# Values of a neighbourhood attention stored per head pair, and attention chunks of every m-th key

## The chip, the cores and the metric

The kernel runs on one core of a Trainium2 chip. The core has a matrix engine (TensorE: the profile has PE for its matmuls and PEld for its weight loads), VectorE (DVE), ScalarE (ACT), GpSimd (POOL), and SyncE (SP), which here issues nearly all transfers; 16 DMA engines carry them out. The metric is the device time of one execution in microseconds (us), the median of the runs.

## The reference, cut to what matters

One encoder layer is applied to a prompt of 256 positions and to a sample of 2048. The mixed positions stand in a grid of rows of 64 columns. Half of the width is a neighbourhood attention with 8 heads of 64 values: each query sees a window of 8 rows and 16 columns, cut out of slabs of keys.

```python
proj = h @ w_in                                   # q, k, v, z_a, u_f, z_f
logits = einsum('bjqhd,bijkhd->bhjqik', q_blk, k_slab) * scale
logits = where(valid, logits + bias, NEG_INF)
p = softmax(logits over all keys of the slab)
out = einsum('bhjqik,bijkhd->bjqhd', p, v_slab)   # y_a
y_f = fourier_mix(u_f, w_fourier, b_fourier)
mixed = concat([rms_norm(y_a, g_na) * silu(z_a), rms_norm(y_f, g_f) * silu(z_f)])
y = x + rms_norm(mixed @ w_out, g_post)
```

All of it is float32. The change lies in how `v` gets from the projection to the last einsum of the attention, and in how `p` is turned for it.

## The kernel before

The kernel has three parts in time. Up to about 600 us it computes the projections and the Fourier half. From 604 to 850 us it computes the attention, and beside it the output product of the Fourier half. The rest is the output product of the attention half, with norm and residual.

*v on its way.* The rows of v of the sample come out of the projection as tiles of 128 positions x 512 values. `put_rows` (L359) stores each of them in the DRAM tensor `vN`, whose layout is [column half, row, column, 512 values]: 16 stores of 128 runs of 2 KB. Six copies from DRAM to DRAM (`v_copy`, L366) then make one tensor `vD` for each of the four column blocks: 23, 31, 31 and 24 columns of the 32 rows, with all 512 values for a key. v of the prompt lies in `vP`, by other stores (L355).

*Passes and groups.* The attention runs in four passes, one for each pair of heads (`pr`, 128 of the 512 values). A pass has nine groups (`group`, L1162): the prompt, and then four row groups R = 0 to 3 with two column halves `hc` each. A group has 256 queries in two blocks `b`; a block sees `NR[R]` rows (11, 15, 15, 12) of a column block's 23, 31, 31 or 24 columns, that is 253 to 465 keys (160 for the prompt). 36 groups in all.

*A group's steps.* `prep` loads its queries four groups ahead. `prep_v` (L1183) loads v and the gate z_a. `scores` (L1211) multiplies queries and keys in PE into `s`; `bias_max` (DVE, L1247), `exps` (ACT, L1252) and `soft` (POOL, L1259) make of it the weights `w`, 128 queries in the partitions and the keys along the free dimension. `transp` (L1571) turns `w` in PE, one chunk of keys at a time, so that the keys stand in the partitions; ACT (L1579) and DVE (L1581) copy the result out of PSUM as `pt`. `pv` (L1586) multiplies it with v, whose keys stand in the partitions too, and DVE (L1607) takes the product to `y`.

*Chunks.* A block of n keys has m = 2, 3 or 4 chunks. Before, chunk x holds the keys z·x to z·x + z − 1, with z = n / m rounded up to a multiple of 8 and at most 128. The load takes the keys of one chunk into the partitions, and the chunks one behind the other in the free dimension: each packet is the 512 B of one key and one head pair, out of the key's 2 KB. Where the rows of `vD` don't reach to m·z keys, the last chunk is a load of its own (L1195; 12 of these, of 84 or 116 keys).

*Order.* PE, DVE, ACT, POOL and SP run in the order of the code, which the loop over k (L1816) writes out by hand. In step k stand the scores of group k, the transposes of group k−1 before and between matmuls of the Fourier half's output (`f_mm`, L1514, or `pairs`), and, late in the step, `pv` of group k−1 (L1907), then `prep_v` of group k+1 (L1917), `prep` of group k+4, and the stores that wait in `puts`. So a group's v is loaded about two steps before `pv` needs it; three buffers hold it (`VB`). All loads and stores of SP are one queue in order: `za`, `ql`, the tables `tb`, the parts `yr` and `yz` for the Fourier half and the stores `oD` and `yD` stand between the loads of v.

Of the kernel before, what the change touches and what calls it, by code (L numbers as in the profile page):

```python
# [10 lines left out]
F32 = mybir.dt.float32  # L11
# [19 lines left out]
K0 = (0, 4, 12, 20)  # L31
KW = (23, 31, 31, 24)
# [142 lines left out]
def build(tc, A, O):  # L175
    nc = tc.nc
# [3 lines left out]
    dr = es.enter_context(tc.tile_pool(name="dr", bufs=1, space=DRAM))  # L180
# [1 line left out]
    qD = dr.tile([4, 128, T], F32, name="qD")  # L182
    kD = dr.tile([4, 128, T], F32, name="kD")

    vD = [dr.tile([32, w, 512], F32, name="vD%d" % i) for i, w in enumerate(KW)]
    vP = dr.tile([2, 4, 40, 512], F32, name="vP")
    zD = dr.tile([2, 512, T], F32, name="zD")
    ZD = dr.tile([128, 16, 512], F32, name="ZD")
    uD = dr.tile([TP, 512], F32, name="uD")

    vN, uN = [dr.tile([2, 32, 32, 512], F32, name=n) for n in ("vN", "uN")]
    sD = dr.tile([5, 128, 4, 512], F32, name="sD")
    xD = dr.tile([7, 128, 4, 512], F32, name="xD")
    ivD = dr.tile([18, 128], F32, name="ivD")
# [5 lines left out]
    ident = cst.tile([128, 128], F32, name="ident")  # L200
# [24 lines left out]
    def mmt(n):  # L225
        x = mmc[0] % 5 > 2
        mmc[0] += 1
        return ps.tile([128, n], F32, tag="t" if x else "a", name="mm", bufs=2 if x else 3)
# [115 lines left out]
    def vu_out(m, c):  # L344
        s, b = PL[c]
        o = st.tile([128, 512], F32, tag="f", name=m + "o", bufs=3)
        x = row_tile(c)
        nc.scalar.activation(o, acc.pop((m, c)), AF.Copy, scale=invt[:, x:x + 1])
        if s is not None:
            put_rows(m, 0, b, s, o)  # L350
        elif m == "u":
            nc.sync.dma_start(uD[c * 128:c * 128 + 128, :], o)
        else:
            for r in range(4):
                nc.sync.dma_start(vP[c, r, 8 * c:8 * c + 32], o[32 * r:32 * r + 32])  # L355
                x = 24 * (1 - c)
                nc.sync.dma_start(vP[1 - c, r, 32 * c:32 * c + 8], o[32 * r + x:32 * r + x + 8])

    def put_rows(m, sg, b, s, o):  # L359
        r = 16 * sg + 4 * s  # L360
        nc.sync.dma_start((vN if m == "v" else uN)[b, r:r + 4].rearrange("r c e -> (r c) e"), o)


    VC = ((0, 0, 0, 23, 0), (1, 0, 8, 24, 0), (1, 1, 0, 7, 24), (2, 0, 24, 8, 0), (2, 1, 0, 23, 8), (3, 1, 8, 24, 0))

    def v_copy(i):  # L366
        x, b, c0, n, d0 = VC[i]
        nc.sync.dma_start(vD[x][:, d0:d0 + n], vN[b][:, c0:c0 + n])


    uu_ = {}
# [125 lines left out]
    def vu(sg, S, hooks):  # L497
# [7 lines left out]
        for i, (j, s) in enumerate(seq):  # L505
            for x in loads.get(i, ()):
                op_load(x)
            if i in splits:
                op_split(splits[i])
            for f in hooks.get(i, ()):  # L510
                f()
            p = mmt(512)
            h, l = op_[j]
            th, tl = bnew[sg, j]
            for k in range(4):
                mm3(nc, p, th[:, k, 128 * s:128 * s + 128], tl[:, k, 128 * s:128 * s + 128], h[k // 2][:, k % 2],
                    l[k // 2][:, k % 2], k == 0, k == 3)
            T2 = lambda o, a: nc.vector.tensor_tensor(out=o, in0=a, in1=p, op=ALU.add)
            if j == 0:
                uc[s] = et("uc")  # L520
                nc.scalar.copy(uc[s], p)
            elif j == 2:
                T2(uc[s], uc[s])
            elif j == 3:
                u4[s] = et("u4")
                T2(u4[s], uc[s])
            else:
                o = st.tile([128, 512], F32, tag="f", name="vuo", bufs=3)
                T2(o, (u4 if j in (4, 6) else uc)[s])
                if j == 4:  # L530
                    T2(uc[s], uc[s])
                put_rows("v" if j in (1, 6) else "u", sg, int(j in (4, 6)), s, o)
# [104 lines left out]
    for kp in range(4):  # L637
        ks = slice(2 * kp, 2 * kp + 2)
        v = part(RV[kp // 2], kp)
# [131 lines left out]
    for b in range(16):  # L771
# [13 lines left out]
        if 2 <= b < 8:  # L785
            x, y = divmod(b, 2)
# [9 lines left out]
        p = mmt(512)[:, :TP]  # L796
# [3 lines left out]
        o = st.tile([128, 256], F32, tag="f", name="f", bufs=3)  # L800
        if kind % 2:
            i, d = p, o
        else:
            i = p.rearrange("p (b r c) -> p b r c", b=2, c=32)
            d = o.rearrange("p (r b c) -> p b r c", b=2, c=32)
# [47 lines left out]
    for i in range(16):  # L853
        sg, pr = divmod(i, 8)
# [14 lines left out]
        o = [st.tile([128, 1024], F32, tag="f", name="f", bufs=3) for x in range(2)]  # L869
# [31 lines left out]
        for j in range(7):  # L901
            for f, d in ((u_load, 0), (u_split, 4), (u_stage1, 6)):
                x = 7 * pr + j - 7 - d
# [33 lines left out]
            if sg == 0:  # L937
                x, y = divmod(7 * (pr - 1) + j, 14)
# [27 lines left out]
            if 9 <= i < 15 and j == 2:  # L966
                v_copy(i - 9)
            p = mmt(512)
# [34 lines left out]
    ptb = [ps.tile([128, 512], F32, tag="t", name="ptb", bufs=2) for i in range(2)]  # L1003
# [179 lines left out]
    def prep_v(g):  # L1183
        cs = slice(g["pr"] * 128, g["pr"] * 128 + 128)
        g["v"] = jl.tile([128, 7, 128], F32, tag="v", name="v", bufs=VB)
        g["ch"], j = [], 0
        for b, (c0, w) in enumerate(g["t"]):
            n = g["nr"] * w
            src = (vP[b] if g["R"] is None else vD[2 * g["hc"] + b][K0[g["R"]]:]).rearrange("r c e -> (r c) e")
            m = -(-n // 128)  # L1190
            z = min(-(-n // m) + 7 & ~7, 128)
            f = m if src.shape[0] >= m * z else n // z
            nc.sync.dma_start(g["v"][:z, j:j + f], src[:z * f, cs].rearrange("(j p) e -> p j e", p=z))
            if f < m:
                nc.sync.dma_start(g["v"][:n - z * f, j + f], src[z * f:n, cs])  # L1195
            ch = [(z * x, min(z, n - z * x), j + x) for x in range(m)]
            g["ch"].append(ch)
            j += len(ch)
        g["za"] = jl.tile([128, 256], F32, tag="za", name="za", bufs=VB)
        nc.sync.dma_start(g["za"], zD[1, cs, g["ts"]])  # L1200

# [69 lines left out]
    for g in G[:2]:  # L1271
        prep(g)
        prep_v(g)
# [11 lines left out]
    for t, (g, x) in enumerate(zip(G, (0, 640))):  # L1285
        g["w"] = []
        for c0, w in g["t"]:
            n = 2 * g["nr"] * w
# [281 lines left out]

    def transp(g, b):  # L1571
        ch = g["ch"][b]
        n, z = len(ch) * 128, ch[0][1]
        o = jp.tile([128, 2, 512], F32, tag="pt", name="pt", bufs=PB)
        for h in range(2):
            for j, (c0, nk, v) in enumerate(ch):
                nc.tensor.transpose(ptb[h][:nk, j * 128:j * 128 + 128], g["w"][b][:, h, c0:c0 + nk], ident)  # L1577
            if h == 0:
                nc.scalar.copy(o[:z, h, :n], ptb[h][:z, :n])  # L1579
            else:  # L1580
                V.tensor_copy(o[:z, h, :n], ptb[h][:z, :n])  # L1581
        g["pt"] = g.get("pt", []) + [o]
# [109 lines left out]
    def part(P, name, n):  # L1692
        return [sm.tile([128, n, 128], F32R, tag="y%s%d" % (x, n) if n < 4 else "y" + x, name="y" + x,
                        bufs=3 if n == 4 else 1) for x in "hl"]
# [103 lines left out]
    prep(G[4])  # L1798
    f_mm(0)
    transp(G[0], 0)  # L1800
    f_norm(range(2))
    transp(G[0], 1)
    soft(G[1], 1)
    run_later()
# [4 lines left out]
    pv(G[0])  # L1809
    ys_load(ftiles[2])  # L1810
    prep_v(G[2])
    split_q(G[3])
    prep(G[5])
    ones32 = sm.tile([128, 32], F32, name="ones32", bufs=1)
    nc.vector.memset(ones32, 1.0)
    for k in range(2, len(G) + 1):  # L1816
        pr, i = divmod(k, 9)
        g, f = G[k] if k < len(G) else None, G[k - 1] if k else None
# [14 lines left out]
        if k == 28:  # L1833
            for c, x in enumerate(("kh", "kl")):
                w = kp.tile([128, T], F32R, tag=x, name="wk")
                WO[c] = [w[:, 56 + D * y:56 + D * y + D] for y in range(2)]
        if k in WK:
            c, y = WK[k]
# [3 lines left out]
        x = k // 2 + 1  # L1842
# [11 lines left out]
        if not g:  # L1854
            a_mm(atiles[0], 0, range(6))
        transp(f, 0)
        if g:
            exps(g, 0, 1)
# [57 lines left out]
        if k + 1 < len(G):  # L1916
            prep_v(G[k + 1])  # L1917
# [123 lines left out]
```

## Time and profile before

| | |
|---|---|
| Median of 3 runs | 959.88 us (959.08 to 960.82) |
| The profiled execution | 958.19 us |
| Its span, first to last instruction | 956.4 us |
| Granted PE clock, mean | 0.997 |
| PE busy (matmuls) | 944.8 us, 99% |
| DVE, ACT, POOL busy | 732.0, 505.8, 453.3 us |
| DMA | 272.17 MB in 140790 packets, mean 285 GB/s |
| Transposes of `w` (L1577) | 440 |

The profile is one execution. Its lines name an engine, an operation, the tiles (out<-in) and the shapes. Weight loads overlap matmuls, so the bars of both add up to more than the time. A line with "x48 | 8.2, 171 | 0.0" stands for 48 instructions, 8.2 us busy, 171 ns each, 0.0 us of idle time before them. "DMA share" is the mean busy share of the 16 DMA engines.

### The profile page before, as it was taken

How to read it: one execution, taken by the hardware profiler on the slowest of the kernel's cores; microseconds unless marked ns; L12 is line 12 of the kernel's file. 1: busy time of each engine (PE TensorE's matmuls, PEld its weight loads, DVE VectorE, ACT ScalarE, POOL GpSimd, SP SyncE). 2: the span in 40 equal slices, each digit the busy share in tenths (PEclk: the TensorE clock that was granted, in tenths of full speed). 3: DMA queues.
4: the chain of work that ended last, by engine and by line, in shares of the span. 5: the costliest groups of instructions: out<-in, count | busy, mean ns of one | idle time of the engine just before them, and what ended most of it. 6: DMA issues, size and time to landing. Idle time of an engine off the chain costs nothing.

```text
span 956.4 us, 16730 instructions
## 1 busy us (share of the span) xinstructions
PE 944.8 (99%) x5595; PEld 784.3 (82%) x5595; DVE 732.0 (77%) x1347; ACT 505.8 (53%) x1088; POOL 453.3 (47%) x426
## 2 busy tenths in 40 slices
PE   9999999999999999999999999999999999999996
PEld 7889988888888888888888879788787888788885
DVE  6758987788876765698887369777888878759876
ACT  6835676433334532233344267677876777654443
POOL 4100002464751302575566045567899798624444
PEclk9999999999999999999999999999999999999998
DMA  9899697557848894499889996698998999889995
GB/s 356 298 385 336 243 339 270 189 201 270 299 188 323 314 341 144 175 352 361 300 289 338 338 341 246 215 276 281 309 253 253 290 280 312 239 296 327 305 317 197
DMA packets 140790, 272.17 MB, mean 285 GB/s; under 512 B 12854, under 2 KB 80664, under 8 KB 137440
## 3 DMA queue, kind: packets, MB, share of 16 engines
q1 hardware_dynamic: 140352, 270.68, 82.9%
q8 instruction: 45, 0.74, 0.3%
q10 hardware_dynamic: 288, 0.40, 0.1%
q14 instruction: 41, 0.34, 0.1%
q0 software_dynamic: 64, 0.02, 0.0%
HBM read 181.37 MB, written 96.81 MB: 291 GB/s over the span
## 4 chain that ended last, share of the span: by engine, by line
PE 89%; DMA 4%; DVE 2%; POOL 2%; ACT 1%; issue 1%; SPq 0%; DVEq 0%; POOLq 0%; ACTq 0%
PE mm L166 18%; PE mm L164 18%; PE mm L165 18%; PE po L1504 10%; PE ptb L1577 5%; PE pv L1593 5%; PE s L1225 4%; DMA yr<-yD 2%; PE px L1689 2%; PE pz L1689 2%; DMA yo<-xt 1%; PE py L164 1%; PE py L165 1%; PE py L166 1%; PE ptb L1043 1%
## 5 line engine op out<-in xcount | busy, mean ns | idle before, releaser
L164 PE MATMUL mm<-xh,wa 128*128 128x512 f32 x448 | 174.4, 389 | 0.0
L166 PE MATMUL mm<-xh,wa 128*128 128x512 f32 x448 | 174.3, 389 | 0.0
L165 PE MATMUL mm<-xl,wa 128*128 128x512 f32 x448 | 174.3, 389 | 0.0
L545 POOL TENSOR_TENSOR ws<-wr 128x512 f32<-128x512 f32 x16 | 22.6, 1415 | 219.3 <-DMA wr<-wz 215.6
L1259 POOL TENSOR_SCALAR w<-w,m 128x465 f32<-128x465 f32 (+9 forms) x136 | 89.3, 670 | 32.7 <-DVE m L1256 13.5
L165 PEld LDWEIGHTS mm<-xl,wa 128*128 128x128 f32 x448 | 84.1, 188 | 17.5
L164 PEld LDWEIGHTS mm<-xh,wa 128*128 128x128 f32 x448 | 84.1, 188 | 17.5
L166 PEld LDWEIGHTS mm<-xh,wa 128*128 128x128 f32 x448 | 84.1, 188 | 17.4
L560 DVE TENSOR_TENSOR wa<-wr,wa 128x512 fp32r<-128x512 f32 x60 | 75.4, 1264 | 21.9 <-ACT wa L559 21.6
L1504 PE MATMUL po<-wk,yh 128*128 128x512 f32 x280 | 87.1, 392 | 0.9 <-ACT yh L1490 0.9
L1252 ACT ACTIVATE w<-w,m 128x465 f32<-128x465 f32 (+9 forms) x136 | 78.4, 579 | 14.3 <-DVE m L1247 13.6
L1968 POOL TENSOR_TENSOR xt<-of,xt 128x512 f32<-128x512 f32 x34 | 43.2, 1293 | 54.6 <-issue 33.0
L1247 DVE CUSTOM_DVE_ANT_1 w<-s,tb 128x465 f32<-128x465 f32 (+8 forms) x124 | 61.4, 529 | 8.9 <-PE s L1225 8.0
L598 POOL TENSOR_TENSOR mt<-mt,rmask 128x880 f32<-128x880 f32 (+2 forms) x24 | 50.3, 2111 | 32.6 <-DVE mt L594 26.2
L164 PE MATMUL mm<-vh,xh 128*128 128x512 f32 x168 | 65.4, 389 | 0.0
L165 PE MATMUL mm<-vl,xh 128*128 128x512 f32 x168 | 65.4, 389 | 0.0
L166 PE MATMUL mm<-vh,xl 128*128 128x512 f32 x168 | 65.4, 389 | 0.0
L1504 PEld LDWEIGHTS po<-wk,yh 128*128 128x128 f32 x280 | 52.1, 188 | 12.2 <-ACT yh L1490 1.3
L891 DVE TENSOR_TENSOR f<-u,mm 128x512 f32<-128x512 f32 x64 | 43.4, 679 | 23.3 <-PE mm L166 18.5
L1577 PE MATMUL ptb<-ident,w 128*120 128x128 f32 (+8 forms) x422 | 59.0, 277 | 1.4 <-ACT pt L1579 1.2
L559 ACT CAST wa<-wr 128x512 fp32r<-128x512 f32 x60 | 36.5, 618 | 43.5 <-PE mm L166 20.4
L1577 PEld LDWEIGHTS ptb<-ident,w 128*120 128x120 f32 (+8 forms) x422 | 47.1, 140 | 14.5 <-issue 4.6
(332 smaller groups left out, 2469.3 us busy)
## 6 DMA issues: line engine op xcount, KB each, us to landing
wr<-wz SPq DMA_DIRECT2D x48, 512.0 KB
vl<-sD SPq DMA_DIRECT2D x20, 512.0 KB
xm<-xm SPq DMA_DIRECT2D x9, 1024.0 KB
oD<-ofs SPq DMA_DIRECT2D x18, 512.0 KB
of<-oD SPq DMA_DIRECT2D x18, 512.0 KB
xt<-xn SPq DMA_DIRECT2D x18, 512.0 KB
yo<-xt SPq DMA_DIRECT2D x35, 256.0 KB
yr<-yD SPq DMA_DIRECT2D x34, 256.0 KB
```

The source lines that it names most:

```text
L164: nc.tensor.matmul(out, lh, rh, start=first, stop=False)
L165: nc.tensor.matmul(out, lh, rl, start=False, stop=False)
L166: nc.tensor.matmul(out, ll, rh, start=False, stop=last)
L560: nc.vector.tensor_tensor(out=o[:, 1], in0=src, in1=o[:, 0].bitcast(F32), op=ALU.subtract)
L598: nc.gpsimd.tensor_tensor(out=o, in0=i, in1=rmask[:, m0:m0 + n].unsqueeze(2).to_broadcast([128, n, 80]), op=ALU.add)
L891: nc.vector.tensor_tensor(out=dst(f, b), in0=src(uu[u]), in1=src(p), op=op)
L1247: nc.vector.tensor_tensor_reduce(out=rows(g["w"][b][:, h, :n], w), in0=rows(g["s"][2 * b + h][:, :nr * sw(w)], sw(w))[:, :, :w], in1=tv, s ...
L1252: nc.scalar.activation(w, w, AF.Exp, bias=m[:, h:h + 1], scale=-1.0, accum_out=m[:, 2 + h:3 + h])
L1259: nc.gpsimd.tensor_scalar(w, w, m[:, 4 + h:5 + h], 1.0, ALU.mult, ALU.mult)
L1504: nc.tensor.matmul(p, (d["l"] if x == 2 else d["h"])[:, c], w(n, int(x == 1), c), start=j == 0, stop=j == 11)
L1577: nc.tensor.transpose(ptb[h][:nk, j * 128:j * 128 + 128], g["w"][b][:, h, c0:c0 + nk], ident)
L1593: nc.tensor.matmul(p[hs, b], g["v"][:nk, v, hs], g["pt"][b][:nk, h, j * 128:j * 128 + 128], start=j == 0, stop=j == len(ch) - 1)
```

## The change

`vN` and `vD` get the head pair as an outer dimension: [column half, 4, row, column, 128] and [4, row, column, 128]. A key's values for one pair are 512 B as before, but the next key's follow directly. `put_rows` stores a tile of v in four runs of 512 B per position. The tensor for u keeps its layout.

Chunk x of a block now holds every m-th key, beginning with key x. Partition p of the load has the keys p·m to p·m + m − 1, which lie side by side in `vD`: a packet has 2 to 4 keys, 1 to 2 KB. The prompt's `vP` isn't changed, and its packets stay at 512 B. The number of partitions is n / m rounded up to an even number, in place of a multiple of 8. There is one load for each block.

The transposes read every m-th column of `w`, and an even number of them, where the tile's width leaves room for the one more (in the first two groups it doesn't always).

```diff
-    vD = [dr.tile([32, w, 512], F32, name="vD%d" % i) for i, w in enumerate(KW)]
+    vD = [dr.tile([4, 32, w, 128], F32, name="vD%d" % i) for i, w in enumerate(KW)]
...
-    vN, uN = [dr.tile([2, 32, 32, 512], F32, name=n) for n in ("vN", "uN")]
+    vN = dr.tile([2, 4, 32, 32, 128], F32, name="vN")
+    uN = dr.tile([2, 32, 32, 512], F32, name="uN")
...
     def put_rows(m, sg, b, s, o):
         r = 16 * sg + 4 * s
-        nc.sync.dma_start((vN if m == "v" else uN)[b, r:r + 4].rearrange("r c e -> (r c) e"), o)
+        if m == "v":
+            nc.sync.dma_start(vN[b, :, r:r + 4].rearrange("h r c e -> (r c) h e"), o.rearrange("p (h e) -> p h e", h=4))
+        else:
+            nc.sync.dma_start(uN[b, r:r + 4].rearrange("r c e -> (r c) e"), o)
...
         x, b, c0, n, d0 = VC[i]
-        nc.sync.dma_start(vD[x][:, d0:d0 + n], vN[b][:, c0:c0 + n])
+        nc.sync.dma_start(vD[x][:, :, d0:d0 + n], vN[b][:, :, c0:c0 + n])
...
             n = g["nr"] * w
-            src = (vP[b] if g["R"] is None else vD[2 * g["hc"] + b][K0[g["R"]]:]).rearrange("r c e -> (r c) e")
             m = -(-n // 128)
-            z = min(-(-n // m) + 7 & ~7, 128)
-            f = m if src.shape[0] >= m * z else n // z
-            nc.sync.dma_start(g["v"][:z, j:j + f], src[:z * f, cs].rearrange("(j p) e -> p j e", p=z))
-            if f < m:
-                nc.sync.dma_start(g["v"][:n - z * f, j + f], src[z * f:n, cs])
-            ch = [(z * x, min(z, n - z * x), j + x) for x in range(m)]
-            g["ch"].append(ch)
-            j += len(ch)
+            z = -(-n // m) + 1 & ~1
+            if g["R"] is None:
+                src = vP[b].rearrange("r c e -> (r c) e")
+                nc.sync.dma_start(g["v"][:z, j:j + m], src[:, cs].rearrange("(p j) e -> p j e", j=m))
+            else:
+                src = vD[2 * g["hc"] + b][g["pr"]].rearrange("r c e -> (r c) e")
+                k0 = K0[g["R"]] * w
+                nc.sync.dma_start(g["v"][:z, j:j + m], src[k0:k0 + z * m].rearrange("(p j) e -> p j e", j=m))
+            g["ch"].append([(x, -(-(n - x) // m), j + x) for x in range(m)])
+            j += m
...
     def transp(g, b):
         ch = g["ch"][b]
-        n, z = len(ch) * 128, ch[0][1]
+        m, z = len(ch), ch[0][1] + 1 & ~1
+        n = 128 * m
         o = jp.tile([128, 2, 512], F32, tag="pt", name="pt", bufs=PB)
         for h in range(2):
             for j, (c0, nk, v) in enumerate(ch):
-                nc.tensor.transpose(ptb[h][:nk, j * 128:j * 128 + 128], g["w"][b][:, h, c0:c0 + nk], ident)
+                y = nk + 1 & ~1
+                y = y if c0 + m * y - m < g["w"][b].shape[2] else nk
+                nc.tensor.transpose(ptb[h][:y, j * 128:j * 128 + 128], g["w"][b][:, h, c0:c0 + m * y - m + 1:m], ident)
```

The order of the instructions hardly moves. On SP's queue, around the loads of v for the two groups of R = 1 in the first pass (steps 2 and 3; sizes are partitions x elements, `vD_64` to `vD_67` the four column blocks), there stood before:

```order
L1193 DMA v<-vD_64 120x3x128
L1193 DMA v<-vD_65 120x4x128
L1200 DMA za<-zD 128x256
L1180 DMA ql<-qD 128x2x128
L1457 DMA oD<-ofs 128x1024
L1457 DMA yD<-y 128x256
L1154 DMA tb<-tD_82 128x1920
L1193 DMA v<-vD_66 120x4x128
L1193 DMA v<-vD_67 120x3x128
```

And now, at the same place:

```order
L1201 DMA v<-vD_64 116x384
L1201 DMA v<-vD_65 118x512
L1205 DMA za<-zD 128x256
L1184 DMA ql<-qD 128x2x128
L1462 DMA oD<-ofs 128x1024
L1462 DMA yD<-y 128x256
L1158 DMA tb<-tD_82 128x1920
L1201 DMA v<-vD_66 118x512
L1201 DMA v<-vD_67 120x384
```

The loads stand where they stood; their partitions and the length of their runs are others. Where a row group has 12 rows (R = 3), the loads of L1195 are gone.

On PE, the transposes of the first of these groups (sizes are those of the output, keys x queries) stood before as:

```order
L1577 MATMUL ptb<-ident,w 120x128 x2
L1577 MATMUL ptb<-ident,w 105x128
L1577 MATMUL ptb<-ident,w 120x128 x2
L1577 MATMUL ptb<-ident,w 105x128
L1504 MATMUL po<-wo_5080,yh 128x512 x2
```

And they stand now as:

```order
L1585 MATMUL ptb<-ident,w 116x128 x6
L1509 MATMUL po<-wo_5080,yh 128x512 x2
L1509 MATMUL po<-wo_5080,yl 128x512
L1509 MATMUL po<-wo_5081,yh 128x512 x2
L1509 MATMUL po<-wo_5081,yl 128x512
```

As many transposes as before, of 116 columns each, at the same place of PE's order.

## The prediction

> **What bounds the kernel now.** I read the page first, then the busy time by stretches, then the waits and the chain of the attention part, where everything that the change touches is used.
>
> ```profile
> span 956.4 us, 16730 instructions
> PE 944.8 (99%) x5595; PEld 784.3 (82%) x5595; DVE 732.0 (77%) x1347; ACT 505.8 (53%) x1088; POOL 453.3 (47%) x426
> ```
> ```profile
> 0.00:604.00 604.00, 602.81 (x2974) 507.29 (x2975) 456.70 (x589) 281.06 (x447) 219.96 (x149) 1.00 0.79 289
> 604.00:850.00 246.00, 244.46 (x2183) 196.96 (x2183) 191.74 (x572) 178.96 (x510) 188.15 (x241) 1.00 0.93 271
> ```
> In the second block each row is a stretch with its length, the busy time of PE, PEld, DVE, ACT and POOL, the granted clock, the busy share of the 16 DMA engines and GB/s. PE sets the time: it is idle for 1.5 of the 246 us of attention (604 to 850). But the DMA engines come second, and closely: 0.93 busy, 0.07 x 246 = 17 us of slack each.
>
> The only wait for v in that stretch's waits (who <- for whom: us, times, longest):
>
> ```profile
> DVE y L1607 <- DMA v<-vD: 1.2, 2, 0.9
> ```
> So v is hardly ever late today. Its lead is read from the loads' issues and from the chain: the third group's load goes out at 614.60 and its product (L1593) starts at 625.84, the fourth's at 618.90 and 633.33.
>
> ```profile
> 614.60 0.97 SPq L1193 DMA_DIRECT2D v<-vD  x2
> ...
> 618.90 1.29 SPq L1193 DMA_DIRECT2D v<-vD  x2
> ```
> ```profile
> 625.84 1.69 PE pv L1593 x28
> 633.33 1.68 PE pv L1593 x28
> ```
> That is a lead of 11 to 14 us, about two groups (246 / 36 = 6.8 us each).
>
> **How a load is shared among the 16 engines.** This carries the forecast. I read the packets "under 512 B" of this stretch as the marks with which each engine ends its share of a transfer, since all loads here have runs of 512 B and more. First 651 to 655.08, in which three transfers of 128 partitions land whole (a fourth is issued 0.85 us before the end, and a fifth after it; they have landed nothing): 48 = 3 x 16.
>
> ```profile
> DMA packets 816, 1.05 MB, mean 257 GB/s; under 512 B 48, under 2 KB 560, under 8 KB 816
> ...
> oD<-ofs SPq DMA_DIRECT2D x1, 512.0 KB
> yD<-y SPq DMA_DIRECT2D x1, 256.0 KB
> yr<-yD SPq DMA_DIRECT2D x1, 256.0 KB
> ```
> ```profile
> 654.23 0.37 SPq L1477 DMA_DIRECT2D yz<-zD  x1
> ```
> Then 823.2 to 837, between two pauses of the DMA engines:
>
> ```profile
> DMA packets 2788, 3.05 MB, mean 221 GB/s; under 512 B 198, under 2 KB 2274, under 8 KB 2786
> ...
> wk<-woD SPq DMA_DIRECT2D x2, 512.0 KB
> gpb<-gpost SPq DMA_DIRECT2D x1, 512.0 KB
> yD<-y SPq DMA_DIRECT2D x1, 256.0 KB
> yr<-yD SPq DMA_DIRECT2D x1, 256.0 KB
> v<-vD SPq DMA_DIRECT2D x2, 128.0 KB
> za<-zD SPq DMA_DIRECT2D x2, 128.0 KB
> v<-vD SPq DMA_DIRECT2D x1, 144.0 KB
> v<-vD SPq DMA_DIRECT2D x2, 58.0 KB
> v<-vD SPq DMA_DIRECT2D x1, 96.0 KB
> v<-vD SPq DMA_DIRECT2D x1, 42.0 KB
> ```
> Fourteen transfers would leave 14 x 16 = 224; there are 198. The eleven of 128 or 96 partitions divide by 16. Left are the two of 58 KB (116 partitions of 512 B) and the one of 42 KB (84 partitions), which must lack 26 shares. If the shares are equal and whole in partitions, 116 goes to 4 engines (29 each) and 84 to 14 (6 each): 2 x 12 + 2 = 26, exactly. So I take it that a load runs on the largest number up to 16 that divides its partitions. [...]
>
> That it is always the same engines the trace shows less well. After the last of the loads, four engines' worth is still at work (0.26 x 16 = 4.2), once after one 58 KB load and once after two:
>
> ```profile
> 706.00:706.50 0.50, 0.50 (x12) 0.50 (x13) 0.39 (x1) 0.50 (x2) 0.50 (x1) 1.00 0.26 68
> 834.75:835.25 0.50, 0.50 (x4) 0.36 (x2) 0.47 (x4) 0.50 (x2) 0.03 (x1) 1.00 0.26 72
> ```
>
> **The change part by part: the loads of v.** Before, a block was cut into chunks of 80 to 128 partitions that are multiples of 8 (the two rests of L1195 apart), so 11 to 16 engines shared it. Now the partitions are what the even rounding gives. Per pass of nine groups, KB on the busiest engines, before and now:
> - 465 keys (4 blocks): 120 partitions of 2 KB on 15 engines, 16 KB each; now 118 on 2 engines, 118 KB each: 4 x 102 more.
> - 345 keys (2): 12 KB; now 116 of 1.5 KB on 4: 43.5; 2 x 31.5 more.
> - 341 keys (2): 12; now 114 on 6: 28.5; 2 x 16.5 more.
> - 372 keys (2): 8 + 14.5; now 124 on 4: 46.5; 2 x 24 more.
> - 276 keys (1): 6 + 3; now 92 on 4: 34.5; 25.5 more.
> - 253, 264, 288, 360 keys and the prompt: the same share (16, 11, 16, 15 and 16 engines).
>
> That is 577.5 KB more per pass on the two busiest engines, 2310 KB (2.37 MB) in four passes. The price of a byte comes from stretches in which the engines are full:
>
> ```profile
> 701.63 0.32 SPq L1457 DMA_DIRECT2D yD<-y  x1
> ```
> ```profile
> 702.50:703.00 0.50, 0.50 (x3) 0.07 (x1) 0.50 (x3) 0.50 (x3) 0.50 (x1) 1.00 1.04 375
> 640.50:641.25 0.75, 0.75 (x6) 0.35 (x4) 0.72 (x4) 0.75 (x3) 0.03 (x1) 1.00 1.04 313
> ```
> The first is the store of y in 2 KB runs: 375 / 1.04 / 16 = 22.5 GB/s per engine. The second is loads of v and y in 512 B runs: 18.8. Runs of 1.5 and 2 KB are nearest to the first. So 2.37 MB / 22.5 = +105 us on these engines. The longer runs give something back: the 0.80 MB of v that each engine moves today fall from 42 us to 35, -7. Net +98; less the slack of 17 us, **+81 us** if all other traffic costs what it costs now. The other end: the other 14 engines are less loaded, so the rest may get quicker too. An engine moves 271 x 246 / 16 = 4.17 MB there, 3.37 without v. At today's mean of 271 / 16 / 0.93 = 18.2 GB/s that is 185 us, at 22.5 it is 150: 150 + 35 + 105 = 290 against 246, **+44 us**. The lead of 11 us is eaten up once, which lowers both; against that, the four groups of a pass that load 465-key blocks carry 471 of its 577.5 KB, and slack of light groups can't be used beyond the lead. I take **+58**: the middle, 62, less 11, and by choice 7 for the unevenness. PE will wait at L1601 (pv), and behind it in PE's order stand the next group's scores, so everything behind is late as well; za, q and y loads on 16 engines each have a share behind the same queue.
>
> **Storing v per head pair.** 16 stores vN<-vo/vuo of 256 KB go out in 512 B runs, not 2 KB: at 18.8 against 22.5 GB/s, 0.87 against 0.73 us per engine, 16 x 0.14 = 2 us of engine time, in a stretch with 0.21 x 604 us of slack: 0, bounds 0 and +2. The six copies vN to vD keep runs of 3.5 KB and more on 128 rows: 0. Twelve issues of SP go away, none of which PE waits for: 0.
>
> **Transposes.** Their number stays 440. Rows by shape, weight loads (mean ns behind the bar's busy us), and six transposes in a row:
>
> ```profile
> L1577 PEld LDWEIGHTS ptb<-ident,w 128*120 128x120 f32 x204 | 23.3, 137 | 8.8 <-issue 3.8 <-POOL w L1259 1.8 <-POOL kl L1141 0.9
> L1577 PEld LDWEIGHTS ptb<-ident,w 128*105 128x105 f32 x48 | 8.2, 171 | 0.0
> L1034 PEld LDWEIGHTS pab<-d,zg 128*32 128x32 f32 x32 | 1.1, 146 | 0.3 <-issue 0.3
> L1551 PEld LDWEIGHTS ptb<-sqs,ones 128*32 128x32 f32 x32 | 0.8, 108 | 0.9 <-issue 0.5 <-DVE sqs L1889 0.3
> L323 PEld LDWEIGHTS ivt<-ident,invt 128*2 128x2 f32 x1 | 0.1, 82 | 0.0
> ```
> ```profile
> L1577 PE MATMUL ptb<-ident,w 128*105 128x128 f32 x48 | 13.1, 273 | 0.0
> ```
> ```profile
> 620.96 0.87 PE L1577 MATMUL ptb<-ident,w 128*120 128x128 f32 x6
> ```
> An odd count costs 34 ns more than a larger even one, but the six, two of them odd, run at (0.87 - 0.273) / 5 = 0.12 us: loads overlap, the pace hides the odd ones. So even counts gain about 0. What every second to fourth column costs no row shows for a transpose; the nearest is L1034, which loads every 8th column: 146 - 82 = 64 ns for 32 columns, against 26 for adjacent ones (L1551), 2.5 times. Low end 0 (hidden under the pace), high end: 120 even columns at (137 - 82) x 2.5 = 137 ns, 17 above the pace, 440 x 17 ns = +8 us; if pairs are lost too (the rate of odd counts, 89 ns for 105), 2.5 x 100 = 250, +130 ns in the 128 with step 4: +17. I take 0, since where the two DMA engines set the time PE has room.
>
> Sum: 958.2 (span 956.4 and 1.8 around it) + 58 = 1016; the median of the runs is 1.7 above the profiled run: **1018 us**.
>
> **The rivals.**
> - *The few engines change from load to load* (not slower). Then the extra is spread, an engine's work per pass stays under 61.5 us, and a 118 KB share takes 5.4 us, inside the lead of 11. For it: the trace's records above only count engines. Against it: two loads in a row leave four engines behind, not eight. It decides wherever a queue never grows past 11 us. Gain: at most PE's idle 1.5 us: 957 to 960. 0.10 (same 0.07, faster 0.03).
> - *Strided weights slow the transposes, with the DMA spread.* +17 us and a little for the step of 3: 978. 0.06. [...]
> - *The forecast*, engines 0 and 1 (as I name the two busiest) set the attention's time: 0.84. Its own range is 958.2 + 44 - 11 + 1.7 = 993 to 958.2 + 81 + 5 + 1.7 = 1046 (5 for transposes or a PE clock that falls in waits; it is 1.00 now).
>
> **How the numbers follow.** A measurement of this kernel can tell about 0.2%, 1.9 us. Slower 0.84 + 0.06 = 0.90, same 0.07, faster 0.03. The range takes in the strided case, 976, and up to 1048; it leaves out the 0.10 that stays near 958 and the far ends.
>
> **What would show it.** In the profile after: the stretch of attention 40 to 80 us longer, PE idle before pv for "DMA v<-vD", a DMA share falling from 0.93 to about 0.7, few engines still busy through waits, most in the groups with 465 keys; time before 604 unchanged. Wrong: PE still 99% busy in that stretch; or transposes paced above 0.12 us, with no waits on v.

## The result, and the profile after

The changed kernel takes 1013.83 us (median of 5 runs, 1012.36 to 1014.12) against 959.43 us before (5 runs, 958.9 to 960.82). The ratio is 1.056, 95% interval 1.0545 to 1.0575: slower by 54.4 us. The forecast was 1018.

From the page after, the span, the busy times and the packets, and then the packets' line of the page before:

```profile
span 1010.8 us, 16720 instructions
PE 963.9 (95%) x5595; PEld 797.4 (79%) x5595; DVE 725.5 (72%) x1347; ACT 508.4 (50%) x1088; POOL 450.7 (45%) x426
DMA packets 130574, 271.98 MB, mean 269 GB/s; under 512 B 12254, under 2 KB 70032, under 8 KB 126904
```
```profile
DMA packets 140790, 272.17 MB, mean 285 GB/s; under 512 B 12854, under 2 KB 80664, under 8 KB 137440
```

The same bytes in fewer packets, and still slower. Where the time went is seen by stretches: up to 604 us, and then from the first `pv` to the last, first after, then before (length, busy PE, PEld, DVE, ACT, POOL, granted clock, DMA share, GB/s).

```profile
0.00:604.00 604.00, 602.37 (x2974) 507.04 (x2975) 455.91 (x589) 281.83 (x447) 220.74 (x149) 1.00 0.80 289
604.90:901.20 296.30, 260.94 (x2181) 210.66 (x2180) 188.44 (x569) 180.52 (x509) 184.70 (x241) 0.94 0.69 220
```
```profile
604.90:850.10 245.20, 243.66 (x2181) 196.60 (x2180) 190.95 (x570) 178.96 (x510) 188.15 (x241) 1.00 0.93 272
```

Ahead of 604 nothing changed, and the first `pv` starts at 604.90 in both. The attention grew from 245.2 to 296.3 us, by 51.1: PE's idle time from 1.5 to 35.4, and its busy time by 17.3 at a granted clock of 0.94 in place of 1.00. The other 3.3 us are in the tail behind the last `pv`. The DMA share fell from 0.93 to 0.69.

PE's waits in this stretch (who <- for whom: us, times, longest):

```profile
PE pv L1601 <- DMA v<-vD: 26.7, 9, 6.0
PE s L1230 <- DVE ofs L1739: 4.7, 4, 1.5
PE ptb L1585 <- ACT pt L1587: 1.7, 2, 1.2
```

The longest of them ends here, before the `pv` of a group with a block of 465 keys; around it stand PE, clock and DMA share by 5 us (the columns are those above), and the last microsecond of the wait:

```profile
716.07 3.26 PE L1601 MATMUL pv<-pt,v 117*64 117x128 f32 x28 [6.02 <-DMA v<-vD]
```
```profile
709.00:714.00 5.00, 1.05 (x5) 0.54 (x3) 2.44 (x5) 0.81 (x3) 2.98 (x3) 1.00 0.88 251
714.00:719.00 5.00, 2.93 (x28) 2.88 (x28) 0.80 (x2) 1.76 (x4) 1.27 (x2) 0.57 0.21 64
719.00:724.00 5.00, 5.00 (x30) 3.90 (x27) 3.74 (x13) 3.52 (x10) 4.92 (x6) 0.74 0.52 185
```
```profile
715.00:716.00 1.00, 0.00 (x0) 0.00 (x0) 0.00 (x0) 0.00 (x0) 0.00 (x0) 0.50 0.15 49
```

At the end of the wait the DMA share is worth 0.15 x 16 = 2.4 engines, which move 49 GB/s, 20 each; the rest stand nearly idle. Around the end of the wait and behind it PE's granted clock is 0.57 and then 0.74. By the nine waits the heavy groups are the late ones: seven of them, 24.2 of the 26.7 us, stand before products of 465-key blocks.

### The profile page after: what moved, and what is told of

It is laid out like the page before. It is cut to its first block, busy times and chain, and to the rows that moved or that the text cites. A ratio compares the mean times of both kernels' runs of the same rounds, so it can differ in the third digit from the quotient of the medians.

```text
span 1010.8 us, 16720 instructions
## 1 busy us (share of the span) xinstructions
PE 963.9 (95%) x5595; PEld 797.4 (79%) x5595; DVE 725.5 (72%) x1347; ACT 508.4 (50%) x1088; POOL 450.7 (45%) x426
## 2 busy tenths in 40 slices
DMA packets 130574, 271.98 MB, mean 269 GB/s; under 512 B 12254, under 2 KB 70032, under 8 KB 126904
## 5 line engine op out<-in xcount | busy, mean ns | idle before, releaser
L1601 PE MATMUL pv<-pt,v 116*64 116x128 f32 (+12 forms) x880 | 62.4, 292 | 26.9 <-DMA v<-vD 26.7
L564 DVE TENSOR_TENSOR wa<-wr,wa 128x512 fp32r<-128x512 f32 x60 | 72.5, 1216 | 20.3 <-ACT wa L563 20.1
L1601 PEld LDWEIGHTS pv<-pt,v 116*64 116x64 f32 (+12 forms) x880 | 51.7, 144 | 40.2 <-issue 33.8
L1585 PEld LDWEIGHTS ptb<-ident,w 128*116 128x116 f32 (+9 forms) x422 | 53.5, 182 | 14.5 <-issue 4.3
L1585 PE MATMUL ptb<-ident,w 128*116 128x128 f32 (+9 forms) x422 | 62.8, 287 | 2.2 <-ACT pt L1587 1.7
```

Source lines behind the costliest of these rows:

```text
L564: nc.vector.tensor_tensor(out=o[:, 1], in0=src, in1=o[:, 0].bitcast(F32), op=ALU.subtract)
L1585: nc.tensor.transpose(ptb[h][:y, j * 128:j * 128 + 128], g["w"][b][:, h, c0:c0 + m * y - m + 1:m], ident)
L1601: nc.tensor.matmul(p[hs, b], g["v"][:nk, v, hs], g["pt"][b][:nk, h, j * 128:j * 128 + 128], start=j == 0, stop=j == len(ch) - 1)
```

## The experiments

The first two questions are whether the sharing is the whole loss, and whether it alone is enough. "Attention" below is the time from the first `pv` to the last in the profiled run.

**e1 and e1b: the change, with all 16 engines for each load.** e1 rounds the partitions of the load up to a multiple of 16 and gives `vD` a 33rd row of keys, so that the loads don't run over the end:

```diff
-    vD = [dr.tile([4, 32, w, 128], F32, name="vD%d" % i) for i, w in enumerate(KW)]
+    vD = [dr.tile([4, 33, w, 128], F32, name="vD%d" % i) for i, w in enumerate(KW)]
...
-        nc.sync.dma_start(vD[x][:, :, d0:d0 + n], vN[b][:, :, c0:c0 + n])
+        nc.sync.dma_start(vD[x][:, :32, d0:d0 + n], vN[b][:, :, c0:c0 + n])
+        nc.sync.dma_start(vD[x][:, 32, d0:d0 + n], vN[b][:, 31, c0:c0 + n])
...
-            z = -(-n // m) + 1 & ~1
+            z = -(-n // m) + 15 & ~15
```

> The changed kernel, but every load of v takes a multiple of 16 partitions (80, 96 or 128), so that all 16 engines share it; layout, every m-th key and even columns stay. Theory (the loads' few engines are the whole loss): no engine has more than its share, PE sets the time again: 956 to 961 us. Rival (the transposes of every m-th column, or the new layout, cost it): stays above 1000; a mixed case would lie between, and what is left above 959 is the price of the layout and the columns.

Measured: 993.06 us, ratio 1.0353 (1.0331 to 1.0375). By the time alone the theory had failed. But the attention took 246.8 us (first `pv` at 634.9, last at 881.7): the loss had gone from there, and 30 us had come in ahead of it. In that part stand the copies to `vD`, two of which read in the list of DMA issues, and some 10 us behind the issue of the first of them by stretches:

```profile
vD<-vN SPq DMA_DIRECT2D x1, 1536.0 KB
vD<-vN SPq DMA_DIRECT2D x1, 1472.0 KB
```
```profile
422.00:424.00 2.00, 2.00 (x10) 1.65 (x10) 2.00 (x2) 0.00 (x0) 1.90 (x1) 1.00 0.22 94
426.00:428.00 2.00, 2.00 (x11) 1.65 (x10) 0.00 (x0) 0.00 (x0) 0.00 (x0) 1.00 0.22 94
```

0.22 x 16 = 3.5 engines at 94 GB/s: a copy of 1.5 MB then takes about 17 us, and SP's loads of `wr` behind it came so late that ACT waited 32.3 us for them. With 32 of 33 rows taken, the copy's 4 x 32 rows no longer lie behind each other, its outermost dimension is 4, and by the 3.5 engines' worth at work I take it that four engines carry it (the count of the marks below, 12778, agrees). That is the sharing of the prediction again, at a place where I had caused it myself. e1b leaves the 33rd row out:

```diff
+                zz = z + 15 & ~15
+                if k0 + zz * m > 32 * w:
+                    zz = z & ~15
+                    nc.sync.dma_start(g["v"][zz:z, j:j + m], src[k0 + zz * m:k0 + z * m].rearrange("(p j) e -> p j e", j=m))
-                nc.sync.dma_start(g["v"][:z, j:j + m], src[k0:k0 + z * m].rearrange("(p j) e -> p j e", j=m))
+                nc.sync.dma_start(g["v"][:zz, j:j + m], src[k0:k0 + zz * m].rearrange("(p j) e -> p j e", j=m))
```

> As e1, but without the added rows: where the rows don't reach (372 and 276 keys, R = 3), the load is split into 112 + 12 or 80 + 12 partitions, so that the copies from vN to vD are again 128 rows that lie behind each other. Theory now (in e1 the 33rd row left the copies only 4 outer rows, so 4 engines carried 1.5 MB each time): the 30 us ahead of the attention go; the attention stays at 247 us from first to last pv: 959 to 963 us, a few us above before for the step in the transposes. Rival (all loads on 16 engines or the layout cost something ahead of the attention): 980 to 995.

Measured: 960.25 us, ratio 1.0019 (1.0009 to 1.0029).

```profile
605.00:851.90 246.90, 245.67 (x2181) 200.32 (x2180) 191.67 (x570) 179.31 (x510) 188.10 (x241) 1.00 0.83 273
```

PE is busy for 245.67 of 246.9 us again. The layout, the step and the even counts all stand in this kernel; only the sharing was mended, and 53 of the 54 us are gone. What remains is 1 to 2 us, and PE's busy time says where: 2.0 us more than before. The DMA share is 0.83 in place of 0.93: the longer packets do save engine time, but nothing here waits for it.

**e5: the kernel before, with the few engines alone.** Only the chunk size is rounded as in the change; layout, runs of 512 B and adjacent columns stay.

```diff
-            z = min(-(-n // m) + 7 & ~7, 128)
+            z = -(-n // m) + 1 & ~1
```

> The kernel before, with only the chunk size rounded to even numbers in place of multiples of 8, and so one load of 118, 116, 114, 124 or 92 partitions: old layout, 512 B runs, adjacent columns. Theory (few engines are enough): 577.5 KB a pass more on two engines, at 18.8 GB/s for 512 B runs 126 us; less slack 17 and lead 0 to 11, or with the other traffic quicker +72 less 11: 1019 to 1068 us, above the changed kernel. Rival (part of the changed kernel's loss is columns or layout): below 1005.

Measured: 1037.65 us, ratio 1.0823 (1.0808 to 1.0838).

```profile
604.70:924.70 320.00, 264.25 (x2181) 210.77 (x2180) 187.55 (x569) 179.78 (x509) 184.31 (x241) 0.93 0.64 201
```

So the partitions alone suffice, and they cost more here, +74.8 us of attention: with the same KB on the busiest engines the attention takes 320.0 us in runs of 512 B and 296.3 in runs of 1.5 and 2 KB. Where two engines set the time, the new layout gives 24 us back.

**e3, e6, e7, e4: the dose.** Four kernels change only how many partitions which load takes, and so the KB on the busiest engines. e3 leaves the even rounding of the load out (253 keys keep 128 partitions, since 127 is a prime):

```diff
-            z = -(-n // m) + 1 & ~1
+            z = -(-n // m) + (n == 253)
```

e6 takes the loads of 465 keys in 128 partitions, e4 in 127:

```diff
-            z = -(-n // m) + 1 & ~1
+            z = 128 if n == 465 else -(-n // m) + 1 & ~1
```
```diff
-            z = -(-n // m) + 1 & ~1
+            z = 127 if n == 465 else -(-n // m) + 1 & ~1
```

e7 is e1b, but with 118 partitions for 465 keys:

```diff
-                zz = z + 15 & ~15
+                zz = z if n == 465 else z + 15 & ~15
```

> The changed kernel, with the loads' partitions not rounded to even numbers (253 keys keep 128): 465 keys now take 117 partitions, which 13 divides, in place of 118, which only 2 divides; 345 keys 115 on 5 engines. One partition less, and the transposes as they are. Theory (largest divisor up to 16): the extra on the busiest engines falls from 577.5 to 8 + 45 + 33 + 48 + 25.5 = 159.5 KB a pass, 29 us of engine time in four passes against 24 of slack and longer runs: 958 to 968 us. Rival (columns or layout): stays at 1010 to 1015.

> The changed kernel, with the loads of 465 keys alone taken in 128 partitions (16 engines). Theory (KB on the two busiest engines add up and only what passes the slack counts): 169.5 KB a pass more are left, 31 us against 24 of slack and longer runs: 958 to 970 us. Rival (each load on few engines is late by itself): the loads of 345, 341, 372 and 276 keys, 7 of 16 in a pass, keep their share of the loss, some 20 us: 975 to 990.

> As e1b, but the loads of 465 keys stay on 118 partitions (2 engines): 408 of the 577.5 KB a pass. Theory (the KB of the two busiest engines add up, whatever load they come from): from 577.5 KB (1013.8 us) to 1121.5 KB (1096.9 us) a KB cost 0.153 us; 169.5 KB less give 988, 978 to 998 us. Rival (the loads of 465 keys carry the whole loss by themselves, since mending them alone gave 961.7): 1008 to 1014 us.

> The changed kernel, with 127 partitions (a prime) in the loads of 465 keys: one engine carries all of the 254 KB. Theory (the same engines each time, and their throughput sets the time): 952 + 169.5 = 1121.5 KB a pass more on engine 0, 204 us in four passes; by the two ends of the prediction +132 to +180, 1090 to 1140 us. Rival (the engines change from load to load, only a load's own duration counts): 254 KB take 11.6 us, about the lead of 11 us, so hardly later than with 118 partitions: 1010 to 1035 us.

The attention of e3, e6, e7 and e4:

```profile
605.20:852.20 247.00, 245.83 (x2181) 200.38 (x2180) 191.53 (x570) 179.19 (x510) 187.97 (x241) 1.00 0.87 269
```
```profile
605.00:851.90 246.90, 245.66 (x2179) 200.32 (x2180) 191.69 (x570) 179.29 (x510) 188.06 (x241) 1.00 0.85 271
```
```profile
605.60:873.40 267.80, 250.96 (x2181) 202.64 (x2180) 190.14 (x570) 180.10 (x510) 186.95 (x241) 0.99 0.76 246
```
```profile
605.00:983.20 378.20, 283.63 (x2180) 229.84 (x2180) 185.46 (x569) 181.25 (x510) 184.18 (x241) 0.85 0.54 174
```

| kernel | KB a pass over the kernel before, where the loads on few engines lie | attention, us | over e1b | median, us | ratio (95%) |
|---|---|---|---|---|---|
| e1b | -24 | 246.9 | 0 | 960.25 | 1.0019 (1.0009 to 1.0029) |
| e3: 465 keys on 13 engines | 159.5 | 247.0 | 0.1 | 960.94 | 1.0028 (1.0017 to 1.0039) |
| e6: 465 keys on 16 | 169.5 | 246.9 | 0.0 | 961.74 | 1.0031 (1.0019 to 1.0043) |
| e7: 465 keys alone on 2 | 384 | 267.8 | 20.9 | 981.75 | 1.0244 (1.0226 to 1.0262) |
| the change | 577.5 | 296.3 | 49.4 | 1013.83 | 1.056 (1.0545 to 1.0575) |
| e4: 465 keys on 1 | 1121.5 | 378.2 | 131.3 | 1096.87 | one run |

The loads of 264 and 372 keys are lighter in e1b than in the kernel before, by 3 + 2 x 10.5 = 24 KB on these engines; e7 has the same loads, so its 408 KB for 465 keys come to 384. All four times lie where the theory had them.

Up to 170 KB nothing is late. From e7 to the change a KB costs 0.15 us (28.5 / 193.5), and from the change to e4 as much (81.9 / 544). The 169.5 KB of the lighter loads cost nothing by themselves (e6), but the change, which differs from e7 in the lighter loads alone, takes 28.5 us more: they lie on the same engines. This speaks against the rival by which the engines change, and e4 does too: 254 KB on one engine should have been hardly worse than 118 KB on each of two, and cost 82 us more. e3 is the shortest proof: one partition less in the loads of 465 keys, 117 = 9 x 13 in place of 118 = 59 x 2, and with 345 keys on 5 engines in place of 4, 53 us are gone.

How full the busiest engines are is an estimate: the 4.17 MB that an engine moves on average in the attention of the kernel before (the prediction's figure) and the change's 2.37 MB make 6.54 MB in 296.3 us, 22 GB/s; for e4 it is (4.17 + 4.59) MB in 378.2 us, 23 GB/s. The prediction's row of full engines has 22.5.

The marks of the transfers ("under 512 B"), read as in the prediction, give the number of engines itself. Counted by the largest divisor up to 16, from the 12854 of before, each kernel should have:

| kernel | by the rule | counted |
|---|---|---|
| the change, and e5 | 12254 | 12254, 12254 |
| e3 | 12438 | 12438 |
| e4 | 12238 | 12238 |
| e6 | 12478 | 12478 |
| e1b | 12970 | 12970 |
| e7 | 12746 | 12746 |
| e1, its copies to `vD` on 4 engines each | 12778 | 12778 |

**e8: a longer lead.** v of group k+2 is loaded at the end of step k, not v of group k+1.

```diff
     prep_v(G[2])
+    prep_v(G[3])
...
-        if k + 1 < len(G):
-            prep_v(G[k + 1])
+        if k + 2 < len(G):
+            prep_v(G[k + 2])
```

> The changed kernel, with v loaded one group earlier (the load for group k+2 is issued at the end of step k; three buffers still do). Theory (the two busiest engines are full, the time is theirs): a longer lead helps once, not in each group: 1000 to 1014 us. Rival (the engines have room, and each load's own 5 to 10 us are too long for the lead): the waits go, 960 to 985.

Measured: 1010.96 us, ratio 1.0553 (1.053 to 1.0577), the attention 296.3 us as in the change, to a tenth. PE's waits in it that add up to more than half a microsecond, and ACT's longest wait, here and then in the change:

```profile
PE s L1230 <- DVE ofs L1739: 12.2, 4, 6.2
PE ptb L1556 <- DVE sqs L1898: 6.7, 3, 4.0
PE ptb L1585 <- ACT pt L1587: 6.5, 4, 2.9
PE po L1509 <- DVE ofs L1541: 6.1, 1, 6.1
PE px L1697 <- ACT ofs L1743: 3.7, 1, 3.7
```
```profile
ACT qh L1209 <- DMA ql<-qD: 56.1, 18, 8.1
```
```profile
ACT qh L1209 <- DMA ql<-qD: 54.4, 19, 7.4
```

PE no longer waits for v at all. It waits for evictions on DVE and ACT instead. ACT stands before loads of queries that are behind v in the queue, but it did so just as long in the change, where PE met the late v first; in the kernel before, no wait for them is listed. The sum is nearly the same: 35.2 us in these five, 33.1 in the three of the change. So the line "DMA v<-vD" was the place where the loss showed, not its cause: all loads of the queue are late, and with v out of PE's way another of them holds it up. That the late queries lie behind these five waits is argued from the queue's order, and not shown link by link.

**e2, e9, e10, e11: the transposes.** Two things of the change, the step and the even counts, taken apart. e2 is the kernel before with the step alone (the turned weights then meet the values of other keys, so it tells of the time only):

```diff
-                nc.tensor.transpose(ptb[h][:nk, j * 128:j * 128 + 128], g["w"][b][:, h, c0:c0 + nk], ident)
+                m = len(ch)
+                y = min(nk, (g["w"][b].shape[2] - 1 - j) // m + 1)
+                nc.tensor.transpose(ptb[h][:y, j * 128:j * 128 + 128], g["w"][b][:, h, j:j + m * y - m + 1:m], ident)
```

e10 is the kernel before with odd counts of adjacent columns:

```diff
-                nc.tensor.transpose(ptb[h][:nk, j * 128:j * 128 + 128], g["w"][b][:, h, c0:c0 + nk], ident)
+                y = nk | 1 if nk < 128 and c0 + nk < g["w"][b].shape[2] else nk
+                nc.tensor.transpose(ptb[h][:y, j * 128:j * 128 + 128], g["w"][b][:, h, c0:c0 + y], ident)
```

e9 is e1b with odd counts, and e11 is e1b with the counts as they fall out:

```diff
-                y = nk + 1 & ~1
+                y = min(nk | 1, 127)
```
```diff
-                y = nk + 1 & ~1
-                y = y if c0 + m * y - m < g["w"][b].shape[2] else nk
+                y = nk
```

> The kernel before, with one thing of the change alone: each transpose reads every m-th column of the weights. Loads, layout and counts are those of before, so the weights are paired with other keys' values: that part of the computation is changed. Theory (few engines): the pace of the transposes hides the slower weight loads, 957 to 961 us. Rival (columns): 1000 and more if they carry the loss, 966 to 976 if they have the price of the prediction's upper bound (+8 to +17).

> As e1b, but the transposes read an odd number of every m-th column wherever the tile's width leaves room. Theory as in the prediction (the pace of the transposes hides it): as e1b, 958 to 962 us. Rival (odd counts at a step don't pair and pass the pace; the +5 us of e2 came from its chunks of 105 and 101 keys, 72 of 440 transposes): 965 to 990 us.

> The kernel before, but the transposes read an odd number of adjacent columns (121, 97, 81 ...) wherever there is room. Theory as in the prediction (even counts gain about 0): 957 to 961 us. Rival (a weight load of 171 ns or more for an odd count sets the pace when all are odd): 965 to 985 us.

> As e1b, but the transposes read the counts as they fall out (117, 116, 116, 116 of 465 keys, 115 three times of 345, 114, 114, 113 of 341), without the even rounding: 104 of the 440 are odd. Theory from e9 (an odd count at a step of 4 costs some 75 to 100 ns more, at a step of 3 some 50): 32 at step 4, 64 at step 3 and 8 at step 2: +5.5 to +6.5 over e1b, 964 to 968 us. Rival (a single odd count between even ones is hidden, as adjacent odd ones are): 958 to 962 us.

Measured: e2 963.9 us, ratio 1.0051 (1.0036 to 1.0067), between the two expectations; e9 979.89, 1.0217 (1.0197 to 1.0236), as the rival had it; e10 960.47, 1.0016 (1.0005 to 1.0027), as the theory had it; e11 964.75, 1.0065 (1.0053 to 1.0077), as expected from e9. The rows show one pattern. Weight loads of e10 (adjacent, odd), of e1b (every 3rd column of 360 keys and every 4th of 465, even) and of e9 (every 4th, 3rd and 2nd column, odd; mean ns behind the bar's busy us), and eight transposes in a row of before, e10, e1b and e9:

```profile
L1578 PEld LDWEIGHTS ptb<-ident,w 128*121 128x121 f32 x188 | 27.1, 183 | 8.0 <-issue 4.2 <-POOL w L1259 1.2 <-POOL kl L1141 0.8
```
```profile
L1589 PEld LDWEIGHTS ptb<-ident,w 128*120 128x120 f32 x48 | 6.3, 186 | 0.7
L1589 PEld LDWEIGHTS ptb<-ident,w 128*118 128x118 f32 x32 | 6.0, 188 | 3.5 <-issue 2.1 <-POOL kl L1145 0.7 <-POOL w L1268 0.3
```
```profile
L1589 PEld LDWEIGHTS ptb<-ident,w 128*117 128x117 f32 x128 | 28.7, 306 | 2.8 <-issue 2.4
L1589 PEld LDWEIGHTS ptb<-ident,w 128*115 128x115 f32 x76 | 13.9, 242 | 3.3 <-issue 2.2 <-POOL ysum L1726 0.6 <-POOL w L1268 0.5
L1589 PEld LDWEIGHTS ptb<-ident,w 128*127 128x127 f32 x12 | 1.6, 196 | 0.4
```
```profile
623.35 1.09 PE L1577 MATMUL ptb<-ident,w 128*120 128x128 f32 x8
```
```profile
623.72 1.14 PE L1578 MATMUL ptb<-ident,w 128*121 128x128 f32 x8
```
```profile
623.69 1.14 PE L1589 MATMUL ptb<-ident,w 128*118 128x128 f32 x8
```
```profile
624.26 1.98 PE L1589 MATMUL ptb<-ident,w 128*117 128x128 f32 x8
```

Adjacent and even, a load of 120 columns takes 137 ns (the prediction's row). An odd count raises that to 183 (121 columns), a step with an even count to 186 (120, every 3rd) or 188 (118, every 4th), and eight transposes get hardly slower by either, 1.09 to 1.14 us: the loads still overlap. A step and an odd count together, 306 ns at a step of 4, are past what the overlap hides, and eight take 1.98 us. So the even rounding of the change is worth something, but only where columns are read at a step: 4.5 us by the medians of e11 and e1b. In e2 the chunks of 105 and 101 keys are odd at a step, which fits its 5 us.

## Why the prediction was right, step by step

- *PE bounds the attention, the DMA engines stand close behind.* Right: with the sharing mended PE is busy for 245.67 of 246.9 us (e1b).
- *A load runs on the largest number of engines up to 16 that divides its partitions.* Right, shown by eight kernels' marks to the last one. The copies of e1, with an outermost dimension of 4, agree: 3.5 engines' worth at 94 GB/s.
- *They are the same engines each time.* Right, shown by the doses adding up, and by e4's 131 us; the rival of engines that change from load to load falls with it. Which of the 16 they are no trace here shows. That the shares of loads on 4 and 6 engines lie on the two busiest as well, as the sum of 577.5 KB has it, was my assumption, which no view of before shows; what the runs showed is that those 169.5 KB cost 0.0 us of attention by themselves (e6) and that the change, which differs from e7 in the lighter loads alone, takes 28.5 more.
- *577.5 KB more a pass, +58 us.* The count stands, and the sum was near: 49.4 us in the attention and 3.3 behind it. The working of the two ends was too wide, though. The upper one, in which all other traffic costs what it did, gives 46 us for e7's 384 KB and 180 for e4; the lower one, in which the rest gets quicker beside idle engines, gives 150 + 35 + 70 - 246 = 9 and 150 + 35 + 204 - 246 = 143. Measured: 20.9 and 131.3. So the lower end holds within 12 us, for the change too (44 against 49.4). The middle that I took, 62, was some 10 too high, and what I took off for the lead covered that by luck: a longer lead left the attention as it was (e8). The price of a KB was too high as well: the sum has 0.18 us (105 / 577.5), the runs show 0.15.
- *The longer runs give back.* Right: between e5 and the change the prediction's terms differ by 126 - 105 + 7 = 28 us, and the attention by 23.7.
- *Storing and copying v: 0.* Right: the first `pv` starts at 604.90 as before.
- *Transposes: 0.* Nearly: e1b keeps 1.7 us of attention over before, with 2.0 more of PE's busy time; the rival at 978, in which they carried the loss, falls with it. But "even counts gain about 0" was taken from adjacent columns, where it holds (e10), and is wrong at a step. The bound of +17, which takes the rate of the odd counts (89 ns for 105 columns), comes near what odd counts cost, but it was worked out for even columns at a step of 4 alone: e9 lost 19.6 us over e1b, at steps of 3 and 4. I had counted it as a risk of the change, and the change's own rounding avoids it. The bounds also set a load's duration against the pace of 0.12 us, and that was too strict: loads of 183 to 188 ns were still hidden.
- *The size of the step.* The prediction had one factor, 2.5, from a step of 8, and for steps of 2 to 4 no row. With even counts a step of 4 costs no more than a step of 3 (188 ns for 118 columns and 186 for 120), and a step of 2 isn't free (80 columns take 155 ns in e1b, 118 in the kernel before). With odd counts the load takes longer the larger the step: 196 ns at a step of 2 for 127 columns, 242 at 3 for 115, 306 at 4 for 117.
- *What would show it.* All of it came: waits for v at `pv`, most of them in the groups with 465 keys, a DMA share of 0.69, some two engines' worth at work at the end of a wait. The clock came on top: 0.94, where the prediction had at most 5 us for it. How much of the 51 us it is by itself was not separated, since with two engines as the bound a slower PE also fills time in which it would have waited.

No version here beats the kernel before. Of those with the new layout e1b comes nearest, 0.2% above it, since PE sets the time and the change takes nothing off PE.

## What to carry to other kernels

Before rounding a tile's partitions, factor the number: by the marks 118 partitions ran on 2 engines and 117 on 13, and a copy in DRAM whose rows no longer lay behind each other had 3.5 engines' worth at work (e1). Where two engines were full, the wait stood where the next load was needed, and loading that one earlier left the attention at 296.3 us (e8); add up KB by engine in place of following the line with the longest wait. A chunk of every m-th key was all right as weights of a transpose with even counts (e1b, ratio 1.0019), and at a step of 3 or 4 a padded column was cheaper than an odd count (186 against 242 ns, 188 against 306).

## What the runs showed of the hardware that I had not expected

- Step and odd count together cost a weight load more than their sum: 137 ns (neither, 120 columns), 183 and 188 (one of them, +46 and +51), 306 (both, at a step of 4, +169).
- With a wait PE's clock fell, and it stayed lower behind it: after 1.00 in the 5 us ahead, it was 0.57 and 0.74 in the 10 us around the end of the 6.02 us one and behind it, and 0.50 in the last microsecond of the wait. With one of 2.02 us it was 0.72 in the 5 us around its end:

```profile
635.75 2.84 PE L1601 MATMUL pv<-pt,v 117*64 117x128 f32 x28 [2.02 <-DMA v<-vD]
```
```profile
634.00:639.00 5.00, 3.02 (x32) 2.65 (x36) 1.05 (x2) 2.09 (x5) 1.60 (x2) 0.72 0.33 104
```

- The issuing queue slows down too. SP's longest issue of two loads of v in the attention, before and then after, and the issue ahead of the long wait and the one within it:

```profile
682.15 3.68 SPq L1193 DMA_DIRECT2D v<-vD  x2
```
```profile
701.93 6.35 SPq L1201 DMA_DIRECT2D v<-vD  x2
711.22 5.24 SPq L1201 DMA_DIRECT2D v<-vD  x2
...
848.35 7.50 SPq L1201 DMA_DIRECT2D v<-vD  x2
```

While SP was at that issue of 5.24 us, the loads behind it in the queue weren't issued, those on 16 engines neither: the `za` behind the issue of 711.22 went out at 716.50. What holds SP there no run here took apart.
